# Hybrid encoder layer on one core: attention biases laid out on the host, values split before scratch, and a list scheduler that counts a shared path

## The chip, the cores and the metric

One core of a Trainium2 chip runs the whole layer. The metric is device time in microseconds (us) of one execution; lower is better. The time before is the median of three runs, 1893.22 us.

Engine names: PE multiplies matrices (PEld is its weight load), DVE is VectorE, ACT is ScalarE, POOL is GpSimd, SP is the engine whose queue issues the DMAs. SBUF is the on-chip memory, PSUM holds the results of PE in eight banks of 512 float32 columns.

## The reference, cut to what matters

Two sequences, p (512 tokens) and s (1024 tokens), pass through one encoder layer with the same weights. Tokens stand on a grid 64 columns wide, so p has 8 rows and s has 16.

```python
n = rms_norm(x, ln1_g) * (1 + sc1) + sh1
z = n @ w_in
q, k, v, xl, gl = jnp.split(z, [D_ATT, 2 * D_ATT, 3 * D_ATT, 3 * D_ATT + D_LRU], axis=-1)
...
# a query (row r, column c) sees 8 rows by 16 columns of keys
bias = rpb[:, dr[None, :, None], dc[:, None, :]]
s = einsum(q, kw) * scale + bias
p = softmax(s); att = einsum(p, vw)
...
# recurrence on xl, forward and backward, with gates; then
x = x + g1 * (concatenate([att, lru]) @ w_out)
x = x + g2 * ((gelu(ug) * uv) @ w_down)   # ug, uv: n2 @ w_up, convolved over tokens
```

There are 8 attention heads of 64, taken in 4 pairs; the feed-forward width is 2816, taken as 22 blocks of 128.

## The kernel before, in words

**Products.** Operands are float32r (a float32 of fewer mantissa bits that PE takes at full rate). Each operand is split into a high part, a copy rounded to float32r, and a low part, the operand less the high part, and a product is three matmuls (`mm3`). A split is thus two instructions per operand, a copy (ACT or DVE) and a subtraction (DVE or POOL), by `split` (line 481).

**Stages.** For each pair of heads, `qkv` (line 907) projects 128 tokens at a time to q, k and v; `lru` (958) does the recurrence; `attend` (1033) does the attention of the pair before, woven in with the projections. This fills about 95 to 851 us, together with the output projection. Then `up` (1331) makes the 22 blocks of the feed-forward inner width by a scheme of seven products for a 2x2 block product, and the down projection (from line 1417) does the same over five chunks of the inner width. In both, the sums of blocks that go into the seven products (`a_terms` 1168, `b_term` 1321) are element-wise work on DVE or POOL, and each sum is split.

**Attention before.** The bias of a pair of heads is read as one table of 16x48 per query place (`tab`, two DMAs of 384 KB for a pair). Twelve masks (0 inside the window, 1e30 outside) are read once per sequence by `masks` (1023). For each of the 8 (s) or 4 (p) query blocks and each head, a subtraction `mask - table window` makes the bias `bi` (lines 1064 to 1066), on DVE or POOL. The values v are copied from PSUM as float32, written to scratch `v_d` in HBM, read back for each column block of keys by `values(cb)` (1047), and there split into high and low part, for both heads:

```python
for hh in range(2):
    R.act(vh[:, :, hh, hh, :], v4[:, :, hh, :], AF.Copy, either=True)
    R.tt(vh[:, :, hh, 1 - hh, :], v4[:, :, hh, :], vh[:, :, hh, hh, :].bitcast(F32), ALU.subtract, pool=None)
```

**The scheduler.** The program is first recorded as a list of operations (`Recorder.op`, line 315) and then put in order by a list scheduler (`_order`, 547). Each engine has a clock; an operation takes its cost from a formula (`tt`: 2.1 ns per element and 150 on POOL, 1.045 and 67 on DVE; `mm`: columns / 2.4 and 2.5 ns). Operations with `pool=None` may go to DVE or POOL, those with `either=True` to ACT or DVE. `leave` (589) decides: an engine gives an operation up where another engine would be done before a share of its own cost is over; the shares are the table `LEAN` (line 39). The order that comes out is fixed in the program; each engine then runs its list in that order. All instructions that `_emit` makes carry line 351 in the profile, so rows are told apart by buffers: `arena_f` and `pieceNF` are float32 SBUF memory, `arena_r` and `pieceNR` float32r SBUF memory, `arena_s` small vectors, `bank` PSUM.

## Time and profile before

| what | value |
|---|---|
| median of 3 runs | 1893.22 us (1892.41 to 1893.79) |
| profiled execution, span | 1892.9 us |
| PE busy | 1721.7 us (91%), 8906 instructions |
| DVE busy | 1495.2 us (79%), 2662 |
| ACT busy | 951.8 us (50%), 1753 |
| POOL busy | 838.9 us (44%), 656 |
| DMA | 201.12 MB, mean 106 GB/s; queue 1 holds 33.2% of 16 engines |

The span is the profiled execution's own time from its first to its last instruction. Busy times of different engines overlap. An engine's busy share is an average over stages that differ, so the stages are read apart: the start (0 to 95 us), projections with attention, recurrence and output projection (95 to 851), up (851 to 1372), down with the last steps of up (1372 to 1893).

### The profile page before, as it was taken

The page shows a single profiled execution, that of the slowest core. Times are in us where ns is not written, and L with a number is a line of the kernel's source. Part 1 is how long each engine was busy: PE and PEld are TensorE (multiplying, and loading weights), DVE is VectorE, ACT ScalarE, POOL GpSimd, SP SyncE. Part 2 cuts the span into 40 slices and gives each one's busy share as a digit, 9 for nine tenths or more (in the row PEclk, how much of TensorE's full clock was granted, in tenths as well). Part 3 has the DMA queues.
Part 4 walks back from the last instruction along what each step waited for, and adds up shares of the span by engine and source line. Part 5 has one row for each costly group of instructions (what it writes and reads, how often), then busy time and mean ns, then how long its engine had stood idle before and what let it go on. Part 6 is the DMA issues. An engine that isn't in the chain of part 4 may idle for free. (4 is left out here: it accounts for less than half of the span.)

```text
span 1892.9 us, 26075 instructions
## 1 busy us (share of the span) xinstructions
PE 1721.7 (91%) x8906; PEld 1416.1 (75%) x8906; DVE 1495.2 (79%) x2662; ACT 951.8 (50%) x1753; POOL 838.9 (44%) x656
## 2 busy tenths in 40 slices
PE   6987979989898899897999999999999888888978
PEld 3665767768687578797888888888887666776756
DVE  5697797897969874868767767667698998789998
ACT  3365863857676741454444444444454554243332
POOL 0364332362616321334333333333255776467874
PEclk9998989999999899998999999999999999999989
DMA  9435314040406465462122221221232331324322
GB/s 369 162 101 150 123 45 134 17 163 13 167 12 189 99 195 173 139 206 79 56 71 64 62 68 62 62 73 56 66 97 81 115 106 55 95 71 143 118 97 97
DMA packets 144695, 201.12 MB, mean 106 GB/s; under 512 B 15793, under 2 KB 83505, under 8 KB 144561
## 3 DMA queue, kind: packets, MB, share of 16 engines
q1 hardware_dynamic: 144560, 199.44, 33.2%
q8 instruction: 70, 1.15, 0.3%
q14 instruction: 65, 0.52, 0.1%
HBM read 157.97 MB, written 41.44 MB: 105 GB/s over the span
## 5 line engine op out<-in xcount | busy, mean ns | idle before, releaser
L351 PE MATMUL bank<-arena_r 128*128 128x512 f32 (+3 forms) x3487 | 859.6, 379 | 58.0 <-ACT piece0F L351 11.0
L351 PEld LDWEIGHTS bank<-arena_r 128*128 128x128 f32 (+1 forms) x3487 | 632.2, 192 | 192.3 <-issue 22.0
L351 PE MATMUL bank<-arena_r,piece0R 128*128 128x512 f32 (+3 forms) x1323 | 325.2, 346 | 8.5 <-DVE piece4F L351 4.4
L351 PEld LDWEIGHTS bank<-arena_r,piece0R 128*128 128x128 f32 (+1 forms) x1323 | 230.6, 194 | 41.5 <-issue 6.3
L351 POOL TENSOR_TENSOR arena_r<-arena_f,arena_r 128x256 fp32r<-128x256 f32 (+4 forms) x172 | 189.8, 1113 | 159.1 <-ACT arena_r L351 74.1
L351 POOL TENSOR_TENSOR arena_f<-arena_f 128x512 f32<-128x512 f32 (+5 forms) x149 | 178.9, 1207 | 99.6 <-issue 42.9
L351 ACT ACTIVATE arena_r<-arena_f 128x256 fp32r<-128x256 f32 (+4 forms) x245 | 115.0, 495 | 130.8 <-PE bank L351 77.8
L351 PE MATMUL bank<-arena_r,piece2R 128*128 128x512 f32 (+1 forms) x735 | 179.5, 335 | 0.0
L351 DVE SCALAR_TENSOR_TENSOR arena_f<-bank,arena_s,arena_f 128x255 f32<-128x255 f32 (+2 forms) x308 | 157.5, 535 | 21.2 <-ACT arena_f L351 10.5
L351 ACT ACTIVATE arena_f<-arena_f,arena_s 128x384 f32<-128x384 f32 (+2 forms) x166 | 101.7, 619 | 84.7 <-DVE arena_s L351 54.4
L351 PEld LDWEIGHTS bank<-arena_r,piece2R 128*128 128x128 f32 x735 | 126.6, 190 | 16.4 <-POOL piece2R L351 0.2
L351 PE MATMUL bank<-arena_r,piece4R 128*128 128x256 f32 (+1 forms) x453 | 137.5, 330 | 0.4 <-DVE arena_f L351 0.4
L351 DVE TENSOR_TENSOR arena_f<-arena_f 128x512 f32<-128x512 f32 (+5 forms) x148 | 134.8, 919 | 3.7 <-ACT arena_f L351 2.5
L351 DVE TENSOR_TENSOR arena_r<-arena_f,arena_r 128x256 fp32r<-128x256 f32 (+5 forms) x143 | 123.8, 882 | 6.6 <-ACT arena_r L351 2.6
L351 ACT ACTIVATE arena_f<-bank 128x512 f32<-128x512 f32 (+3 forms) x186 | 82.3, 454 | 75.1 <-DVE bank L351 36.9
L351 PE MATMUL bank<-piece0R,arena_r 128*128 128x512 f32 (+3 forms) x316 | 104.4, 398 | 2.1 <-DVE arena_s L351 2.0
L351 ACT ACTIVATE piece0R<-arena_f 128x512 fp32r<-128x512 f32 (+2 forms) x78 | 48.9, 627 | 113.1 <-PE bank L351 92.5
L351 ACT ACTIVATE arena_f<-bank,arena_s 128x512 f32<-128x512 f32 (+1 forms) x132 | 89.6, 683 | 24.5 <-PE bank L351 15.2
L351 DVE TENSOR_TENSOR bank<-bank,arena_f 128x512 f32<-128x512 f32 (+1 forms) x89 | 52.3, 589 | 51.3 <-PE bank L351 32.8
L351 PEld LDWEIGHTS bank<-arena_r,piece4R 128*128 128x128 f32 x453 | 83.5, 190 | 9.3 <-issue 0.8
L351 ACT ACTIVATE piece2R<-arena_f 128x512 fp32r<-128x512 f32 x63 | 39.8, 631 | 89.9 <-PE bank L351 77.9
L351 DVE SCALAR_TENSOR_TENSOR arena_f<-arena_f,arena_s 128x511 f32<-128x511 f32 (+3 forms) x102 | 70.9, 696 | 17.4 <-ACT arena_f L351 15.4
(432 smaller groups left out, 3214.1 us busy)
## 6 DMA issues: line engine op xcount, KB each, us to landing
arena_f<-in_w_up_dram SPq DMA_DIRECT2D x96, 256.0 KB
gd<-arena_f SPq DMA_DIRECT2D x62, 256.0 KB
piece2F<-in_ada_dram SPq DMA_DIRECT2D x18, 512.0 KB
arena_f<-in_w_qkv_dram SPq DMA_DIRECT2D x24, 384.0 KB
arena_f<-gd SPq DMA_DIRECT2D x39, 192.0 KB
piece3F<-in_ada_dram SPq DMA_DIRECT2D x14, 512.0 KB
arena_f<-gd SPq DMA_DIRECT2D x46, 128.0 KB
arena_f<-in_ada_dram SPq DMA_DIRECT2D x8, 512.0 KB
```

Of the source, the lines that this page charges most:

```text
L351: fn(**{k: (v.real() if isinstance(v, View) else v) for k, v in kw.items()})
```

## The change

Three parts.

1. The host lays out the whole bias, -1e30 outside the window, as `bias_p` [4 pairs, 4 blocks, 128, 2 x 256] and `bias_s` [4, 8, 128, 2 x 384]. `attend` reads one tile per query block (256 KB for p, 384 KB for s, 48 DMAs in all), in place of 16 table DMAs and 12 mask DMAs with their 12 copies, and of 96 subtractions. The sign moves into the softmax (`scale=-1.0`).
2. `qkv` writes the values to scratch already split, [H | L | L | H] in 256 columns, from PSUM. `values` reads them straight into matmul operands. That takes away the 64 copies and 64 subtractions of `values` and adds 48 subtractions out of PSUM on DVE; the 48 copies out of PSUM stay, in another form. The scratch traffic doubles.
3. The scheduler has a resource `port`: an operation on POOL, and one on DVE whose operands are all in SBUF (other than tensor_reduce and reciprocal), starts there no earlier than the last such operation ended. `leave` compares ends with that in mind, and `LEAN` is gone. The cost of a float32r matmul becomes columns / 2.4 + 13.5 ns, at least 109.

```diff
-LEAN = {("DVE", "POOL"): 0.389, ("DVE", "DVE"): 0.536, ("ACT", "ACT"): 0.611, ("ACT", "DVE"): 1.869, ("DVE", "ACT"): 1.004}
+ONE_PORT = ("tensor_reduce", "reciprocal")
...
         o.all = {eng: (cost, emit), **dict(alts)}
+        o.port = {"POOL"} if eng == "POOL" or "POOL" in alts else set()
+        if port:
+            o.port.add("DVE")
...
-        self.op("DVE", per * n + base + (60 if ps else 0), self._emit(getattr(self.nc.vector, name), kw), reads, w, alts=alts)
+        self.op("DVE", per * n + base + (60 if ps else 0), self._emit(getattr(self.nc.vector, name), kw), reads, w, alts=alts, port=not ps and name not in ONE_PORT)
...
-            self.op("DVE", *b, [in0, in1], [out], alts={"POOL": a} if pool is None else {})
+            self.op("DVE", *b, [in0, in1], [out], alts={"POOL": a} if pool is None else {}, port=not self._ps(out, in0, in1))
...
-            cost = max(64.0, n) / 2.4 + 2.5 if rhs.ap.dtype == F32R else max(214.0, n / 0.6)
+            cost = max(max(64.0, n) / 2.4 + 13.5, 109.0) if rhs.ap.dtype == F32R else max(214.0, n / 0.6)
...
         def leave(o, e, s):
+            own = (max(s, port) if e in o.port else s) + o.alts[e][0]
             for f, (cost, _) in o.alts.items():
                 if f != e:
                     ahead = sum(ops[p].all[f][0] for c, p, v in ready[f] if c < o.key and not stale(c, p, v, f))
-                    if max(clock[f], s) + ahead + cost < s + LEAN[o.first, e] * o.alts[e][0]:
+                    if max(clock[f], s, port if f in o.port else s) + ahead + cost < own:
                         return True
             return False
...
             o.cost, emit = o.all[e]
+            if e in o.port:
+                s = max(s, port)
+                port = s + o.cost
...
-                vt = R.buf([P, 2, P], F32, "vt")
+                vt = R.buf([P, 2, 4, 64], F32R, "vt")
...
-                    R.copy(vt[:, u, :], pt[:, 256:384], either=True)
+                    v2 = pt[:, 256:384].rearrange("p (h d) -> p h d", h=2)
+                    R.act(vt[:, u, 0:4:3, :], v2, AF.Copy, either=True)
+                    R.tt(vt[:, u, 1:3, :], v2, vt[:, u, 0:4:3, :].bitcast(F32), ALU.subtract)
...
         def values(cb):
-            vr, vh = R.buf([P, nck, P], F32, "vr"), R.buf([P, nck, 2, 2, 64], F32R, "vh")
+            vh = R.buf([P, nck, 2 * P], F32R, "vh")
             for a in range(nck):
-                R.dma(vr[:, a, :], src[a, :, KB[cb]:KB[cb] + 32, :])
-            v4 = vr.rearrange("p a (h d) -> p a h d", h=2)
-            for hh in range(2):
-                R.act(vh[:, :, hh, hh, :], v4[:, :, hh, :], AF.Copy, either=True)
-                R.tt(vh[:, :, hh, 1 - hh, :], v4[:, :, hh, :], vh[:, :, hh, hh, :].bitcast(F32), ALU.subtract, pool=None)
+                R.dma(vh[:, a, :].bitcast(F32), src[a, :, KB[cb]:KB[cb] + 32, :])
             return vh
...
+                bi = R.buf([P, 2, nk], F32, "bi")
+                R.dma(bi, {"p": bias_p, "s": bias_s}[q][j, var])
                 for hh in range(2):
-                    bi = R.buf([P, nk], F32, "bi")
-                    R.tt(bi.rearrange("p (a b) -> p a b", b=32), msk[var].rearrange("p (a b) -> p a b", b=32), tbs[hh][:, a0:a0 + nr, b0:b0 + 32], ALU.subtract, pool=None)
...
-                    R.vec("tensor_tensor_reduce", e, [pS[hh], bis[hh]], in0=pS[hh], in1=bis[hh], scale=1.0, scalar=3e38, op0=ALU.add, op1=ALU.min, accum_out=mn)
+                    R.vec("tensor_tensor_reduce", e, [pS[hh], bi[:, hh, :]], in0=pS[hh], in1=bi[:, hh, :], scale=-1.0, scalar=3e38, op0=ALU.add, op1=ALU.min, accum_out=mn)
```

What the scheduler makes of it is seen only in the engines' lists. Counted over the whole program, POOL goes from 661 instructions to 499, DVE from 2664 to 2690, ACT from 1635 to 1588, SP's queue from 765 to 785; PE keeps 8764. By the part of the program that records an operation, the element-wise work on POOL goes from 187 operations to 60 in the projections, the recurrence and the attention of all pairs of heads but the last, from 145 to 84 in up, and from 266 to 303 in down. In down, DVE goes from 493 operations to 423 and ACT from 345 to 378.

On POOL, in the attention and recurrence of one pair of heads of s (`128x384` are the bias subtractions, `128x4x64` the value splits, `128x1024` the products and sums of the recurrence, `128x768` the splits of weights); before:

```order
L351 TENSOR_TENSOR arena_r<-arena_f,arena_r 128x768 x3
L351 TENSOR_TENSOR arena_f<-arena_f,piece3F 128x384 x6
L351 TENSOR_TENSOR piece1R<-piece3F,piece1R 128x4x64
L351 TENSOR_TENSOR arena_f<-piece2F,piece3F 128x384
L351 TENSOR_TENSOR piece2F<-piece2F,arena_s 128x512
L351 TENSOR_TENSOR arena_f<-piece2F,piece3F 128x384 x2
L351 TENSOR_TENSOR piece3F<-arena_f,piece3F 128x384
L351 TENSOR_TENSOR arena_r<-piece4F,arena_r 64x1024
L351 TENSOR_TENSOR piece2F<-piece2F,piece4F 128x1024 x2
L351 TENSOR_TENSOR piece4F<-piece4F,piece2F 128x1024
L351 TENSOR_TENSOR piece4F<-piece4F,piece3F 128x1024
L351 TENSOR_TENSOR piece1R<-piece4F,piece1R 128x4x64 x2
```

and in the changed program, between the same kinds of weight splits of a pair:

```order
L352 TENSOR_TENSOR arena_r<-arena_f,arena_r 128x768 x2
L352 TENSOR_TENSOR piece2F<-piece2F,arena_s 128x512
L352 TENSOR_TENSOR arena_r<-arena_f,arena_r 128x256 x2
L352 TENSOR_TENSOR arena_r<-piece2F,piece0R 128x512
L352 TENSOR_TENSOR arena_r<-arena_f,arena_r 128x768 x3
L352 TENSOR_TENSOR piece0R<-arena_f,arena_r 128x768
L352 TENSOR_TENSOR piece4F<-piece4F,arena_s 128x512
```

The bias and value instructions are gone from POOL, and the `128x1024` ones of the recurrence stand on DVE.

On DVE, in a step of up (`128x512` from arena and piece to arena_r or piece4R are splits of weights, those on `bank` the sums out of PSUM); before:

```order
L351 TENSOR_TENSOR arena_r<-arena_f,piece0R 128x512
L351 TENSOR_TENSOR arena_f<-arena_f 128x512
L351 TENSOR_TENSOR piece4R<-arena_f,piece2R 128x512
L351 TENSOR_TENSOR bank_70<-bank_70,arena_f 128x256
L351 TENSOR_TENSOR bank_72<-bank_72,arena_f 128x256
L351 TENSOR_TENSOR bank_69<-bank_69,arena_f 128x512
L351 TENSOR_TENSOR bank_71<-bank_71,arena_f 128x512
```

and now:

```order
L352 CAST arena_r<-arena_f 128x512
L352 TENSOR_TENSOR arena_r<-arena_f,arena_r 128x512
L352 TENSOR_TENSOR bank_71<-bank_71,arena_f 128x256
L352 TENSOR_TENSOR bank_73<-bank_73,arena_f 128x256
L352 CAST piece4R<-arena_f 128x512
L352 TENSOR_TENSOR bank_70<-bank_70,arena_f 128x512
L352 TENSOR_TENSOR arena_r<-arena_f,piece4R 128x512
L352 TENSOR_TENSOR bank_72<-bank_72,arena_f 128x512
L352 CAST piece4R<-arena_f 128x512
L352 TENSOR_TENSOR arena_r<-arena_f,piece4R 128x512
```

In up, DVE takes 62 copies of 512 columns from ACT and 61 subtractions from POOL, and they stand between its sums out of PSUM.

## Rows read from the trace of the kernel before

**Rows 1.** Windows by stage: length, busy us (instructions) of each engine, clock, DMA

```profile
core 0: us, PE busy (x) PEld busy (x) DVE busy (x) ACT busy (x) POOL busy (x), PEclk, DMA share, GB/s
0.00:95.00 95.00, 76.17 (x352) 46.52 (x353) 56.65 (x151) 35.77 (x57) 22.08 (x25) 0.93 0.72 265
95.00:851.00 756.00, 680.77 (x3695) 557.93 (x3694) 603.69 (x1293) 456.08 (x839) 293.41 (x210) 0.95 0.38 120
851.00:1372.00 521.00, 509.24 (x2948) 449.98 (x2947) 371.52 (x586) 243.94 (x426) 189.14 (x131) 0.99 0.22 65
1372.00:1893.00 521.00, 455.48 (x1917) 361.64 (x1915) 463.37 (x635) 216.01 (x433) 334.28 (x291) 0.96 0.31 98
```

**Rows 2.** Waits of PE, 95 to 851 us: us in total, times, longest

```profile
PE bank L351 <- DVE arena_r L351: 13.3, 11, 3.6
PE bank L470 <- issue: 8.5, 1, 8.5
PE bank L351 <- ACT piece2F L351: 7.2, 2, 5.2
...
PE bank L351 <- DVE piece0R L351: 0.6, 1, 0.6
```

**Rows 3.** Windows of one slice: two of attention, one of up, one of down

```profile
473.00:520.00 47.00, 39.56 (x235) 32.11 (x236) 46.28 (x115) 30.10 (x72) 30.07 (x23) 0.96 0.49 167
520.00:568.00 48.00, 47.40 (x254) 39.32 (x252) 32.81 (x57) 35.19 (x54) 9.44 (x4) 1.00 0.05 13
1041.00:1088.00 47.00, 47.00 (x270) 41.40 (x269) 33.43 (x58) 22.11 (x38) 16.12 (x11) 1.00 0.21 62
1750.00:1797.00 47.00, 42.35 (x174) 33.29 (x174) 46.23 (x54) 15.78 (x34) 37.79 (x30) 0.96 0.39 120
```

**Rows 4.** Timeline of DVE, 1000 to 1012 us: start, duration (us), instruction

```profile
1000.40 0.74 DVE L351 SCALAR_TENSOR_TENSOR arena_f<-bank,arena_s,arena_f 128x511 f32<-128x511 f32 x1
1001.08 1.33 DVE L351 TENSOR_TENSOR piece4R<-arena_f,piece0R 128x512 fp32r<-128x512 f32 x1
1002.33 1.78 DVE L351 TENSOR_TENSOR arena_f<-arena_f 128x512 f32<-128x512 f32 x1
1005.18 0.69 DVE L351 TENSOR_TENSOR arena_r<-arena_f,piece0R 128x512 fp32r<-128x512 f32 x1 [1.08 <-ACT piece0R L351]
```

**Rows 5.** Timeline of POOL, the same stretch

```profile
1000.56 3.00 POOL L351 TENSOR_TENSOR arena_f<-arena_f 128x512 f32<-128x512 f32 x2 [0.63 <-DVE arena_f L351]
1009.47 1.29 POOL L351 TENSOR_TENSOR piece4R<-arena_f,piece2R 128x512 fp32r<-128x512 f32 x1 [5.91 <-ACT piece2R L351]
```

**Rows 6.** Groups of DVE, 95 to 851 us: count, busy us, mean ns, idle before

```profile
L351 DVE TENSOR_SCALAR arena_f<-arena_f,arena_s 128x384 f32<-128x384 f32 x33 | 25.3, 775 | 0.2
...
L351 DVE TENSOR_TENSOR arena_f<-arena_f 128x384 f32<-128x384 bf16 x8 | 6.5, 820 | 0.1
...
L351 DVE COPY arena_f<-bank 128x128 f32<-128x128 f32 x22 | 6.0, 280 | 2.5 <-ACT piece2F L351 1.9 <-ACT piece4F L351 0.6
...
L351 DVE TENSOR_TENSOR piece2F<-arena_f 128x384 f32<-128x384 bf16 x1 | 0.5, 546 | 0.0
```

**Rows 7.** Groups of DVE, 710 to 757 us, where POOL has three instructions

```profile
L351 DVE TENSOR_TENSOR arena_f<-arena_f,piece4F 128x1024 f32<-128x1024 f32 x1 | 1.2, 1227 | 0.0
```

**Rows 8.** Groups of DVE, 0 to 47 us

```profile
L351 DVE CAST piece1R<-piece2F 128x512 fp32r<-128x512 f32 x2 | 0.8, 424 | 0.9 <-ACT piece2F L351 0.9
```

**Rows 9.** Waits of PE, 851 to 1372 us

```profile
PE bank L351 <- DVE piece4F L351: 8.1, 1, 8.1
```

**Rows 10.** Waits of PE, 1372 to 1893 us

```profile
PE bank L351 <- ACT arena_f L351: 18.0, 5, 8.0
PE bank L351 <- ACT piece0F L351: 11.0, 6, 3.9
PE bank L351 <- DVE bank L351: 10.5, 6, 2.2
```

**Rows 11.** Who waited for the table DMAs of the biases

```profile
  POOL arena_f L351: 5.1, 1
  POOL arena_r L351: 4.6, 1
```

More of the change, by code (lines that the diff above doesn't have):

```diff
@@ L208 @@
 class Op:
-    __slots__ = ("pos", "eng", "cost", "lat", "emit", "deps", "left", "users", "ready", "bufs", "aset", "start", "end", "vt", "done", "name", "alts", "all", "win", "ver", "key", "first", "move", "late", "strict")
+    __slots__ = ("pos", "eng", "cost", "lat", "emit", "deps", "left", "users", "ready", "bufs", "aset", "start", "end", "vt", "done", "name", "alts", "all", "win", "ver", "key", "first", "move", "late", "strict", "port")
 class Recorder:
@@ L312, in fixed_view, with op @@
         return self.dram(t, "fixed")
-    def op(self, eng, cost, emit, reads, writes, aset=None, lat=0.0, also=(), alts=(), move=0.0):
+    def op(self, eng, cost, emit, reads, writes, aset=None, lat=0.0, also=(), alts=(), move=0.0, port=False):
         o = Op()
@@ L372, in act @@
             alts["DVE"] = (1.045 * self._n(in_) + 127 if self._ps(in_) else 0.523 * self._n(in_) + 67, self._emit(self.nc.vector.tensor_copy, dict(out=out, in_=in_)))
-        self.op("ACT", cost, self._emit(self.nc.scalar.activation, kw), [in_, scale, bias], [out, accum_out], aset=SETS.get(func), alts=alts)
+        self.op("ACT", cost, self._emit(self.nc.scalar.activation, kw), [in_, scale, bias], [out, accum_out], aset=SETS.get(func), alts=alts, port=either and not self._ps(out, in_))
     def _act(self, out, in_, scale=None):
@@ L743, in encoder @@
 def encoder(ctx: ExitStack, tc: tile.TileContext, x_p, x_s, c_t, ada, bada, lng, w_qkv, w_xg,
-            qkg, tab, mask, lruv, gatew, w_out, w_up, w_down, ffv, y_p, y_s):
+            qkg, bias_p, bias_s, lruv, gatew, w_out, w_up, w_down, ffv, y_p, y_s):
     nc = tc.nc
@@ L790, in encoder @@
     g_d = scratch([NH, P, TP + TS], "gd")
-    v_d = {q: [scratch([s["T"], P], f"vd{q}{j}") for j in range(4)] for q, s in seqs.items()}
+    v_d = {q: [scratch([s["T"], 2 * P], f"vd{q}{j}") for j in range(4)] for q, s in seqs.items()}
     def rsqrt(ss, n, scale):
@@ L1021, in lru, with attend @@
         R.dma(cat_d[q][4 + c], h)
-    def masks(q):
-        nv, mcols, moff = (4, 256, 0) if q == "p" else (8, 384, 4 * 256)
-        out = []
-        for v in range(nv):
-            raw, m = R.buf([P, mcols], F32, "mkr"), R.buf([P, mcols], BF16, "msk")
-            R.dma(raw, mask[:, moff + v * mcols:moff + (v + 1) * mcols])
-            R.copy(m, raw)
-            out.append(m)
-        return out
-    def attend(q, msk, j, kqs):
+    def attend(q, j, kqs):
         kh, kl, qs = kqs
@@ L1293, in encoder @@
             pq, pj, pk = prev
-            if n in (1, 5):
-                msk = masks(pq)
-            weave(main, nmain, attend(pq, msk, pj, pk), 7 if pq == "p" else 15)
+            weave(main, nmain, attend(pq, pj, pk), 7 if pq == "p" else 15)
         prev = (q, j, out[0]) if out else None
@@ L1573, in _layout @@
     rpb = a["rpb"][0]
-    r, c = np.arange(8), np.arange(16)
-    ra = np.clip((np.arange(TAB_R) - 4)[None, :] - r[:, None] + 7, 0, 14)
-    cb = np.clip((np.arange(TAB_C) - 16)[None, :] - c[:, None] + 15, 0, 30)
-    t = rpb[:, ra[:, None, :, None], cb[None, :, None, :]]
-    f["tab"] = t.reshape(4, 2, P, TAB_R * TAB_C).transpose(0, 2, 1, 3)
-    f["mask"] = _masks()
+    table = np.concatenate([rpb.reshape(8, 15 * 31), np.full((8, 1), -BIG, np.float32)], axis=1)
+    for q, at in zip("ps", _places()):
+        t = table[:, at]
+        f["bias_" + q] = t.reshape(4, 2, *at.shape).transpose(0, 2, 3, 1, 4)
     cols = [a["lru_conv_w"][0][i] for i in range(4)] + [a[n][0] for n in ("lru_conv_b", "lam_f", "lam_b")]
@@ L1595, in _layout @@
     return f
-_ORDER = ["x_p", "x_s", "c_t", "ada", "bada", "lng", "w_qkv", "w_xg", "qkg", "tab", "mask", "lruv", "gatew",
+_ORDER = ["x_p", "x_s", "c_t", "ada", "bada", "lng", "w_qkv", "w_xg", "qkg", "bias_p", "bias_s", "lruv", "gatew",
           "w_out", "w_up", "w_down", "ffv"]
```

40 lines of the change are left out of this document (17 added, 23 removed).

## The prediction

> **What bounds the kernel now.** I read the windows by stage first, then the waits of PE in each stage, then single slices, then the timeline where DVE and POOL run together. The profiled execution spans 1892.9 us, 0.3 under the median of 1893.2, so the sum is made against the span and 0.3 is added at the end. PE is the engine with the most work, 1721.7 us busy, but it is not equally full. In up it is busy 509 of 521 us; from 95 to 851 it is idle for 756 - 681 = 75 us, and in down for 521 - 455 = 66 us [rows 1]. What the change can win lies in these two.
>
> From 95 to 851 the waits of PE itself add to 74.5 us. Ten rows name DVE, from 13.3 to 0.6 us, together 50.8; five name ACT, together 14.8, the largest 7.2; one of 8.5 names nothing [rows 2]. So two thirds of the idle time hang on DVE. Slices show how: where DVE is busy 46.3 of 47 us, PE gets 39.6; in the next slice DVE is busy 32.8 of 48 and PE 47.4. In up, DVE at 33.4 of 47 leaves PE without a gap [rows 3]. DVE near 70% is harmless, DVE near 98% costs PE about 7 us per slice.
>
> Much of DVE's busy time is no work. On the timeline an SBUF-only subtraction of 512 columns takes 1.33 and then 1.78 us while POOL works, and 0.69 when POOL is still; a DVE instruction that reads PSUM, beside the same POOL instruction, takes its 0.74 [rows 4]. POOL's two take 3.00 us, 1.5 each, where one alone takes 1.29 [rows 5]. So the two engines take turns on SBUF, while DVE's work out of PSUM goes on beside POOL. This is what the change now tells its scheduler.
>
> **The attention stretch, 95 to 851 us.** DVE has 150 SBUF-only groups there, 808 instructions, 438 us busy; the first has 33 at 775 ns, the last one at 546 ns, whose form elsewhere averages 820 [rows 6]. If each is priced at the fastest twentieth of its form in the trace, they need 293 us, which leaves 145 of waiting. With the least mean of a form's groups as price it would be 81, which is the low end, since those groups wait too; the high end is POOL's own 293 us there [rows 1]. I take 145: single instructions show the price best.
>
> POOL keeps 60 of 187 operations in this part. Waiting goes with POOL's instructions, so two thirds of it should go: -98 us of DVE's time. DVE's own work changes as follows. Gone: 38 bias subtractions, 30 of 384 columns at 0.55 [rows 6] and 8 shorter ones, 20 us; 25 copies and 24 subtractions of values and 12 mask copies at about the 0.28 of a 128-column copy [rows 6], 17. Added: 48 subtractions out of PSUM at 0.28, 13; 22 operations of 1024 columns from POOL at 1.23 [rows 7], 27; 18 of 512 at 0.69 [rows 4], 12; 5 of 768 at about 0.95, between the two, 5. The balance is +20. DVE would then be busy 604 - 98 + 20 = 526 of 756 us, 70%, which is the share that left PE full in up. Of the 50.8 us that hang on DVE I count 35 as gone: the chain of softmax and recurrence keeps some. The ends are 0 and the whole 75.
>
> The granted clock adds to this. It is 0.95 on average in this stretch and 1.00 in the slice where PE waits least [rows 1, 3]. With the two levels of 1.2 and 2.4 GHz, 0.95 means that a tenth of the 756 us ran at the lower, which costs 38 us of PE's work. I count half of that back, 19 us; ends 0 and 38. The Trainium skill, "TensorE: Matmul & The Clock Gate", section "HAM oscillation", says that PE's clock drops in its waits, so that the work behind a wait runs slower too, and that an order which keeps PE busy keeps the clock. By that rule alone the whole 38 would come back with the waits; the slices agree in direction, 0.96 beside 39.6 us busy and 1.00 beside 47.4.
>
> The transfers grow: 48 bias tiles (16.8 MB) for 8.4 MB of tables and masks, and twice the 9.4 MB of scratch traffic of the values, so about 18 MB more. Over 756 us that is 24 GB/s on top of 120, at a DMA share of 0.38 [rows 1]. I price it at nothing: the cover is the idle 0.62 of the queues, and the table DMAs made two waits of 5 us in all, on POOL [rows 11]. Without that cover each of the 48 would be waited for, at the 265 GB/s of the start [rows 1] 1.0 us for 256 KB and 1.5 for 384 KB: 16 + 48 = 64 us at most. SP's queue issues in order, so a bias tile that waits for free memory also holds the weight loads behind it; that is in this upper end. A gain here is left out, as only 10 us of waits named the tables, and on POOL.
>
> **Up, 851 to 1372 us.** PE is full but for 12 us, 8.1 of which is a single wait for DVE at the entry [rows 9]. DVE takes 62 copies at 0.42 [rows 8] and 61 subtractions at 0.69, 68 us in all, onto 372 [rows 1], and sheds part of its waits, since POOL gives up 61. That is at most 440 of 521, 84%. I put 0; the cover is DVE's remaining sixth. Ends -8 and what the slower rival gives.
>
> **Down, 1372 to 1893 us.** Here DVE is busy 463 and POOL 334 of 521 us [rows 1], in the worst slice 46.2 and 37.8 of 47 [rows 3], and PE waits for copies on ACT (18.0, 11.0) and sums on DVE's banks (10.5) that come late [rows 10]. The change gives POOL 37 operations more, DVE 70 less, ACT 33 more. The SBUF time that DVE and POOL share stays about equal: what leaves DVE for POOL costs more there, what leaves it for ACT costs it nothing. So this stage gains by order alone: PSUM work of DVE is set beside POOL's turns by a plan that knows of them. I take -12, a fifth of PE's 66 idle us; ends -45 (two thirds) and +22 (below).
>
> The matmul cost of 13.5 ns changes only when the scheduler believes PE to be free; it moves nothing that I can price, and is in the width of down.
>
> **Sum.** -35 (waits) - 19 (clock) + 0 (transfers) + 0 (up) - 12 (down) = -66: 1892.9 - 66 + 0.3 = 1827 us.
>
> **The rivals.**
>
> *Down gains as well.* If the plan sets down as I set the best end, -45 in place of -12: 1794 us. For it: the stage has the longest waits between DVE and POOL. Against: the shared time is not less. Chance 0.12; the forecast itself 0.52, with a range of its own of 1795 to 1858.
>
> *Down gives back.* POOL holds SBUF for 1.29 us per 512 columns where DVE would for 0.69 [rows 4, 5]; 37 operations more on POOL then lengthen the shared time by up to 37 x 0.6 = 22 us, in a stage where it is the limit. Attention gains 54, down loses 22: 1861 us. The Trainium skill, "SBUF — State Buffer", section "Who interferes with whom", says that the pair of ports is locked for a whole instruction and the loser blocks fully. By that rule the slower engine should never be given work where the pair is the bound, and the price is the full 22; the timeline agrees that a DVE instruction waits out POOL's. Chance 0.17.
>
> *VectorE becomes the wall in up: slower.* In the new list of DVE, copies and subtractions of weights stand in pairs between the sums out of PSUM. A sum that stands behind two of them is late by 1.1 us, and PE's banks with it. This decides once DVE's slices in up come over 46 of 47 us; then PE would get what it gets in down at that share, 42.4 of 47 [rows 3], and up loses 521 x 0.10 = 51 us. The rest would keep half of its gain with a VectorE that full, 33: 1893 + 51 - 33 = 1911 us. For it: +68 us of work there, and ACT, half idle, loses work. Against: 84% is not 98%. Chance 0.14.
>
> *The change does not do what it says.* The old shares may already have kept the two engines apart as well as a list in fixed order can; POOL's remaining instructions are the long ones, and the waits stay while DVE gets 20 us more and loses some chains. That leaves 1893 us. Chance 0.05.
>
> **How the numbers follow.** A difference under 0.2% (3.8 us) is about what a measurement of this kernel cannot tell from no change. Faster: 0.52 + 0.12 + 0.17 = 0.81; same 0.05; slower 0.14. The range of 1775 to 1900 holds the forecast, both milder and better cases and no change; it leaves out the slower rival and the far end of a good down stage.
>
> **What would show it.** POOL's instructions near 494 in the trace and its busy time in the attention stretch near 100 us; DVE's busy time there near 530, with 512-column subtractions close to 0.7 us; PE idle there near 40 us, clock 0.97; up still 509 to 521 busy; down with PE idle near 54. The forecast is wrong if DVE's slices in up are full, if PE waits for `in_bias` or scratch DMAs, or if down grows longer than 521 us.

## The result and the profile after

The changed kernel takes 1824.34 us (median of four runs, 1821.89 to 1826.37) against 1893.51 for the kernel before: ratio 0.9637, 95% interval 0.9623 to 0.965. The profiled execution spans 1822.5 us. The forecast was 1827 us, within 1775 to 1900.

The page of the changed kernel, span and busy time of each engine:

```profile
span 1822.5 us, 25666 instructions
PE 1705.3 (94%) x8906; PEld 1412.9 (78%) x8906; DVE 1421.5 (78%) x2688; ACT 927.2 (51%) x1706; POOL 619.8 (34%) x494
```

PE has the same 8906 matmuls. Its busy time fell by 16.4 us (1721.7 to 1705.3) and its idle time by 54 (1892.9 - 1721.7 = 171.2 before, 117.2 now). These two are the whole gain of 70.4.

Windows of the changed kernel at the boundaries of [rows 1] (the last is shorter), with the same columns:

```profile
0.00:95.00 95.00, 80.20 (x427) 54.73 (x428) 60.78 (x184) 46.27 (x76) 14.32 (x15) 1.00 0.73 265
95.00:851.00 756.00, 705.11 (x3881) 586.43 (x3880) 578.81 (x1287) 468.17 (x844) 155.29 (x97) 0.95 0.46 149
851.00:1372.00 521.00, 516.47 (x2927) 452.61 (x2925) 387.02 (x717) 211.28 (x366) 96.09 (x70) 1.00 0.22 66
1372.00:1823.00 451.00, 403.54 (x1674) 319.12 (x1674) 394.90 (x503) 201.49 (x422) 354.06 (x313) 0.96 0.33 104
```

These windows no longer hold the same work: 3881 matmuls fall in 95 to 851 us where 3695 did. So I set the boundaries again where the same matmul starts, counted from the end. The stages are then attention (95 us to the first matmul of the output projection of s), output projection, up, and down. Windows of the kernel before, at these boundaries:

```profile
95.00:713.00 618.00, 547.78 (x2947) 441.70 (x2946) 518.86 (x1160) 400.90 (x754) 252.32 (x186) 0.95 0.35 110
713.00:867.00 154.00, 146.56 (x864) 129.60 (x863) 100.76 (x151) 64.88 (x101) 51.14 (x31) 0.98 0.49 159
867.00:1497.00 630.00, 611.21 (x3364) 532.71 (x3363) 466.90 (x765) 298.56 (x538) 252.13 (x199) 0.98 0.23 71
1497.00:1893.00 396.00, 339.93 (x1388) 265.54 (x1386) 352.07 (x440) 151.68 (x306) 261.25 (x217) 0.96 0.31 99
```

and of the changed kernel:

```profile
95.00:673.00 578.00, 533.15 (x2873) 434.25 (x2872) 448.27 (x1097) 390.07 (x717) 97.64 (x60) 0.94 0.46 148
673.00:823.00 150.00, 145.59 (x861) 129.41 (x860) 105.82 (x160) 64.69 (x104) 40.93 (x27) 0.99 0.52 171
823.00:1440.00 617.00, 609.36 (x3364) 528.87 (x3364) 462.86 (x824) 258.00 (x455) 141.24 (x108) 1.00 0.21 66
1440.00:1823.00 383.00, 337.02 (x1389) 265.63 (x1387) 343.78 (x426) 168.18 (x358) 325.63 (x285) 0.96 0.35 109
```

- Attention is 40 us shorter. PE's idle time falls from 70.2 to 44.8 us. The rest is mostly that 75 matmuls more are done before 95 us (427 against 352), at a granted clock of 1.00 in place of 0.93.
- The output projection gains 4 us, up 13 (PE idle 18.8 to 7.6), down 13 (56.1 to 46.0).
- The clock in attention did not rise: 0.95 and 0.94.

Waits of PE, 95 to 851 us, changed kernel (us in total, times, longest), beside [rows 2]:

```profile
PE bank L352 <- ACT piece2F L352: 10.1, 2, 8.9
PE bank L352 <- ACT piece3F L352: 5.8, 2, 4.7
PE bank L471 <- ACT piece2F L352: 5.7, 2, 4.9
PE bank L352 <- DVE arena_s L352: 3.8, 5, 1.6
```

The largest row on DVE fell from 13.3 us to 3.8; the largest of all now names ACT. Over the same work, from 95 us to the first matmul of up, the rows that name DVE fall from 53.2 us in all to 16.7, and those that name ACT rise from 15.0 to 31.3. The 48 bias tiles delay nobody: the list under the last line is empty for those of s, shown here, and for those of p. All instructions on the bias of s:

```profile
L352 SPq DMA_DIRECT2D arena_f<-in_bias_s_dram x31: 327/422/1188, 264.9 to 561.7; - x31
L352 SPq DMA_DIRECT2D piece2F<-in_bias_s_dram x1: 482/482/482, 451.5 to 451.5; - x1
its engine sat idle before it (us, times) until:
who waited for it (us, times):
```

### The profile page after: what moved, and what is told of

Read it like the earlier page. It is cut to its first block, busy times and chain, and to the rows that moved or that the text cites. A ratio compares the mean times of both kernels' runs of the same rounds, so it can differ in the third digit from the quotient of the medians.

```text
span 1822.5 us, 25666 instructions
## 1 busy us (share of the span) xinstructions
PE 1705.3 (94%) x8906; PEld 1412.9 (78%) x8906; DVE 1421.5 (78%) x2688; ACT 927.2 (51%) x1706; POOL 619.8 (34%) x494
## 2 busy tenths in 40 slices
DMA packets 147571, 218.91 MB, mean 120 GB/s; under 512 B 16113, under 2 KB 82289, under 8 KB 147441
## 4 chain that ended last, share of the span: by engine, by line
PE 68%; DVE 12%; ACT 6%; DMA 5%; issue 5%; POOL 3%; SPq 2%; ACTq 0%; DVEq 0%; POOLq 0%
PE bank L352 65%; DVE arena_f L352 4%; DVE arena_r L352 3%; PE bank L471 2%; SPq L352 2%; DVE piece2F L352 2%; ACT arena_f L352 2%; POOL arena_r L352 1%; DVE arena_s L352 1%; ACT piece2F L352 1%; DVE piece3F L352 1%; ACT arena_r L352 1%; DMA arena_r<-vdp 1%; DVE piece4F L352 1%; ACT piece3F L352 1%
## 5 line engine op out<-in xcount | busy, mean ns | idle before, releaser
L352 PE MATMUL bank<-arena_r 128*128 128x512 f32 (+4 forms) x4169 | 995.5, 370 | 44.8 <-ACT piece0F L352 9.1
L352 PEld LDWEIGHTS bank<-arena_r 128*128 128x128 f32 (+1 forms) x4169 | 732.4, 192 | 188.8 <-issue 21.5
L352 POOL TENSOR_TENSOR arena_f<-arena_f 128x512 f32<-128x512 f32 (+3 forms) x144 | 170.8, 1191 | 432.8 <-DVE arena_f L352 173.6
L352 DVE SCALAR_TENSOR_TENSOR arena_f<-bank,arena_s,arena_f 128x511 f32<-128x511 f32 (+1 forms) x310 | 159.7, 538 | 28.1 <-ACT arena_f L352 20.1
L352 PE MATMUL bank<-arena_r,piece0R 128*128 128x512 f32 (+3 forms) x669 | 174.2, 366 | 1.8 <-ACT piece3F L352 1.1
L352 ACT ACTIVATE arena_f<-arena_f,arena_s 128x384 f32<-128x384 f32 (+3 forms) x190 | 115.3, 621 | 98.6 <-DVE arena_f L352 71.4
L352 PE MATMUL bank<-piece0R,arena_r 128*128 128x512 f32 (+5 forms) x479 | 140.6, 381 | 1.7 <-DMA arena_r<-vdp 0.8
L352 PEld LDWEIGHTS bank<-arena_r,piece0R 128*128 128x128 f32 (+1 forms) x669 | 121.1, 194 | 25.5 <-issue 7.2
L352 DVE TENSOR_TENSOR arena_r<-arena_f,arena_r 128x512 fp32r<-128x512 f32 (+5 forms) x147 | 125.2, 858 | 15.6 <-ACT arena_r L352 13.1
L352 DVE TENSOR_TENSOR arena_f<-arena_f 128x512 f32<-128x512 f32 (+4 forms) x120 | 94.8, 801 | 14.6 <-ACT arena_f L352 11.4
L352 DVE TENSOR_TENSOR bank<-bank,arena_f 128x512 f32<-128x512 f32 (+1 forms) x89 | 52.0, 587 | 23.2 <-PE bank L352 14.7
L352 DVE SCALAR_TENSOR_TENSOR arena_f<-arena_f,arena_s 128x511 f32<-128x511 f32 (+3 forms) x102 | 57.3, 562 | 11.5 <-ACT arena_f L352 10.0
```

What stands on the lines that cost most here:

```text
L352: fn(**{k: (v.real() if isinstance(v, View) else v) for k, v in kw.items()})
```

## The experiments

Two theories stood against each other. **Waits**, the prediction's own: PE idles because VectorE waits for the SBUF path behind GpSimd; take those waits away and PE's idle time goes. **Plan**: the waits cost little by themselves. What costs is that the order was made by a scheduler that does not know of them, so its instructions stand in a wrong order on each engine.

### The scheduler alone, the data alone

`sched_only` is the kernel before with part 3 of the change only; biases and values are as before.

```diff
-LEAN = {("DVE", "POOL"): 0.389, ("DVE", "DVE"): 0.536, ("ACT", "ACT"): 0.611, ("ACT", "DVE"): 1.869, ("DVE", "ACT"): 1.004}
+ONE_PORT = ("tensor_reduce", "reciprocal")
...
+            if e in o.port:
+                s = max(s, port)
+                port = s + o.cost
...
-            cost = max(64.0, n) / 2.4 + 2.5 if rhs.ap.dtype == F32R else max(214.0, n / 0.6)
+            cost = max(max(64.0, n) / 2.4 + 13.5, 109.0) if rhs.ap.dtype == F32R else max(214.0, n / 0.6)
```

> The kernel before with part 3 alone: the shared path in the clocks and in the choice of engine, no table of shares, the new matmul cost; biases and values as before. POOL keeps 180 of 187 operations in the attention part, 84 in up, 297 in down. Theory A (what the scheduler knows of the shared path wins the time): most of the 69 us, 1840 to 1855 us. Theory B (the work taken out of attention wins it, the scheduler does little): 1875 to 1890 us. Theory C (both needed, since with the biases and splits still there the path stays loaded in attention): 1855 to 1875, with the gain in up and down (some 25 us) there and attention as long as before.

Measured 1846.71 us, ratio 0.9755 (0.9733 to 0.9778): 47 us of the 69, as theory A had it.

`data_only` has parts 1 and 2 with the old scheduler: the changed kernel with these lines reversed.

> The changed kernel with the scheduler of before (table of shares, no shared path, matmul cost of 2.5 ns): parts 1 and 2 alone. POOL has 107 operations in the attention part, 146 in up, 274 in down. Theory A: at most 20 us of gain, 1873 to 1890 us. Theory B: 1825 to 1845 us. Theory C: 1845 to 1865 us, the gain of some 35 us in attention, with up and down as before.

Measured 1911.98 us, ratio 1.0093 (1.0077 to 1.011): slower, by 18 us, outside all three expected ranges. So with the scheduler of before, fewer instructions and less work on GpSimd (187 operations in attention before, 107 here) bring nothing in this order.

### Without the waits

`no_pool` is the changed kernel in which every operation with a choice between VectorE and GpSimd stays on VectorE.

```diff
-            self.op("DVE", *b, [in0, in1], [out], alts={"POOL": a} if pool is None else {}, port=not self._ps(out, in0, in1))
+            self.op("DVE", *b, [in0, in1], [out], alts={}, port=not self._ps(out, in0, in1))
```

> The changed kernel with every choice between DVE and POOL settled for DVE, so nothing can wait for the shared path. DVE then has 1147 operations in attention (1082 in the changed kernel), 930 in up (817), 761 in down (423). Theory: attention and up stay within 10 us, since DVE has room there, and DVE's SBUF instructions run at their own length (0.69 us for 512 columns); down becomes DVE's: 303 more operations at 0.4 to 0.7 us are some 150 us on top of about 270 of its own work, 420 us or more in place of 382, so 1850 to 1880 us in all. Rival (POOL does more harm than good everywhere): under 1815 us.

Measured 1961.7 us, ratio 1.0363 (1.0347 to 1.0378): both expectations missed. Down did not become the problem (398 us, where 420 or more was expected); attention and up, which were to stay within 10 us, grew by 37 and 89. Their windows:

```profile
95.00:710.00 615.00, 542.45 (x2900) 439.26 (x2899) 464.77 (x1171) 384.36 (x709) 0.00 (x0) 0.93 0.44 138
858.00:1564.00 706.00, 645.60 (x3362) 541.44 (x3362) 507.03 (x990) 243.08 (x423) 0.00 (x0) 0.96 0.19 58
```

GpSimd does nothing in attention, so VectorE waits for nobody on SBUF; it is busy 76% (464.77 of 615). PE is idle 72.5 us there, about as long as before the change (70.2). Up is 89 us longer than in the changed kernel though VectorE is busy only 72% there. The prediction had read from one good slice that 70% is harmless; it is not so in itself.

`no_port` is the changed kernel whose scheduler takes the two engines as independent, with the new matmul cost.

```diff
-                    if max(clock[f], s, port if f in o.port else s) + ahead + cost < own:
+                    if max(clock[f], s) + ahead + cost < s + o.alts[e][0]:
...
-            if e in o.port:
-                s = max(s, port)
-                port = s + o.cost
```

> The changed kernel, but the scheduler takes DVE and POOL as independent (no table of shares either; an operation goes where it ends first). It tells the shared path in the plan from the mere loss of the table and from the new matmul cost. Theory A: the plan's knowledge is what pays, so 1845 to 1875 us, the loss mostly in down, where both engines are loaded. Rival: the table of shares was what held the kernel back, and the path in the plan is worth nothing: 1820 to 1830 us.

Measured 1913.75 us, ratio 1.0113 (1.0098 to 1.0128): slower than theory A's 1845 to 1875, and the rival's 1820 to 1830 is refuted.

How long VectorE waits shows in what the same operation takes. Two groups of VectorE in attention (busy us, mean ns, idle before): 66 TENSOR_TENSOR operations on 16 columns, the same in every kernel, and TENSOR_SCALAR operations on 384 columns. In `before`, `sched_only`, the changed kernel, `no_port` and `no_pool`, one fence each:

```profile
L351 DVE TENSOR_SCALAR arena_f<-arena_f,arena_s 128x384 f32<-128x384 f32 x33 | 25.3, 775 | 0.2
...
L351 DVE TENSOR_TENSOR arena_s<-arena_s 128x16 f32<-128x16 f32 x66 | 21.1, 320 | 0.4
```

```profile
L354 DVE TENSOR_TENSOR arena_s<-arena_s 128x16 f32<-128x16 f32 x66 | 21.7, 329 | 0.3
...
L354 DVE TENSOR_SCALAR arena_f<-arena_f,arena_s 128x384 f32<-128x384 f32 x35 | 15.3, 441 | 0.2
```

```profile
L352 DVE TENSOR_TENSOR arena_s<-arena_s 128x16 f32<-128x16 f32 x66 | 13.9, 211 | 0.7
...
L352 DVE TENSOR_SCALAR arena_f<-arena_f,arena_s 128x384 f32<-128x384 f32 x26 | 10.7, 412 | 0.1
```

```profile
L352 DVE TENSOR_SCALAR arena_f<-arena_f,arena_s 128x384 f32<-128x384 f32 x35 | 17.5, 504 | 0.3
...
L352 DVE TENSOR_TENSOR arena_s<-arena_s 128x16 f32<-128x16 f32 x66 | 13.6, 206 | 0.7
```

```profile
L352 DVE TENSOR_SCALAR arena_f<-arena_f,arena_s 128x384 f32<-128x384 f32 x31 | 12.9, 415 | 0.4
...
L352 DVE TENSOR_TENSOR arena_s<-arena_s 128x16 f32<-128x16 f32 x66 | 11.3, 171 | 0.7
```

One group does not stand for all: `sched_only` has the 16-column operations as before (329 and 320 ns), but the 384-column ones almost as fast as `no_pool` (441 and 415, 775 before). So here is an estimate over all of VectorE's instructions in attention that touch SBUF alone: the time that each takes beyond the fastest twentieth of the same operation and shape in all fourteen kernels' traces, added up. Beside it stand the rows of PE's waits there that name DVE and ACT, each added up (all in us; `long_plan` is explained further down):

| kernel | VectorE waits (estimate) | PE waits for DVE | PE waits for ACT | attention |
|---|---|---|---|---|
| before | 109 | 46.0 | 14.7 | 618 |
| sched_only | 64 | 26.7 | 25.1 | 589 |
| changed kernel | 37 | 16.4 | 27.2 | 578 |
| no_port | 35 | 38.0 | 30.3 | 629 |
| long_plan | 33 | 53.4 | 23.3 | 630 |
| no_pool | 7 | 24.0 | 44.1 | 615 |

VectorE's waits do not set the length of attention. `no_port` and `long_plan` have those of the changed kernel (35 and 33, and 37), yet PE waits for VectorE two and three times as long and attention takes 51 and 52 us more. `no_pool` has next to none and stands at 615. **Waits** falls as the main cause. `sched_only` does not decide between the theories, since VectorE waits 45 us less in it: the scheduler that knows of the path also makes an order with fewer waits on it. Windows of attention of `sched_only`:

```profile
95.00:684.00 589.00, 536.69 (x2884) 430.07 (x2883) 465.99 (x1078) 407.95 (x775) 208.76 (x191) 0.94 0.36 114
```

and of `no_port`:

```profile
95.00:724.00 629.00, 559.77 (x2926) 444.48 (x2925) 469.92 (x1161) 388.98 (x713) 83.85 (x50) 0.93 0.43 137
```

VectorE is as busy in both (466 and 470 us), and GpSimd works 2.5 times as long in the shorter one. The largest row of PE's waits in `no_port`, 95 to 724 us, beside 3.8 us in the changed kernel:

```profile
PE bank L352 <- DVE arena_s L352: 17.3, 7, 6.7
```

### Each term of the scheduler

`port_only` is the kernel before with the shared path and without `LEAN`, matmul cost 2.5 ns as before (`sched_only` without its last two diff lines).

> The kernel before with the shared path in its scheduler and without the old shares, but with the old matmul cost of 2.5 ns. Its plan ends at 1738 us; the changed kernel with the old matmul cost ended 131 us after its plan. Theory (both terms are needed for a plan that holds): 1738 + 131 = about 1869, between 1855 and 1880, so half or less of the 46.7 us that both terms gave on the data of before. Rival A (the shared path alone is the gain): 1847. Rival B (the matmul cost alone): 1893.

Measured 1855.93 us, ratio 0.9808 (0.9792 to 0.9825): 37.7 us, four fifths of what both terms give on this data. That is just inside the expected range, but "half or less" was wrong. `LEAN` goes with the path in this run: no run on this data tells the two apart.

`old_mm_cost` is the changed kernel with the matmul cost of before.

```diff
-            cost = max(max(64.0, n) / 2.4 + 13.5, 109.0) if rhs.ap.dtype == F32R else max(214.0, n / 0.6)
+            cost = max(64.0, n) / 2.4 + 2.5 if rhs.ap.dtype == F32R else max(214.0, n / 0.6)
```

> The changed kernel with the old cost of a matmul in the scheduler (2.5 ns instead of 13.5 over the columns). After the first four runs the theory is: what pays is that the scheduler's clocks agree with the chip, be it on the shared path or on PE, since leaving out the shared path alone costs 90 us (1914) though less waits there. Theory A (the shared path is the part that matters): within 15 us of the changed kernel, 1820 to 1840. Theory A2 (PE's cost matters as much): 1850 to 1880, the loss in attention and up, where PE would be believed 5% faster than it is.

Measured 1880.71 us, ratio 0.9934 (0.9917 to 0.995): at the upper end of theory A2, 56 us slower than the changed kernel, 32 of them in attention (610 and 578) and 12 in the output projection. The timeline of PE shows which cost is right. Changed kernel, 999 to 1004 us (start, duration, instruction), where nothing is waited for:

```profile
999.68 0.62 PE L352 MATMUL bank<-piece3R,piece4R 128*128 128x512 f32 x2
1000.13 0.39 PE L352 MATMUL bank<-piece3R,arena_r 128*128 128x512 f32 x1
1000.36 0.62 PE L352 MATMUL bank<-arena_r,piece4R 128*128 128x512 f32 x2
1000.81 0.39 PE L352 MATMUL bank<-arena_r 128*128 128x512 f32 x1
1001.04 0.40 PE L352 MATMUL bank<-arena_r,piece4R 128*128 128x256 f32 x2
...
1002.11 0.40 PE L352 MATMUL bank<-arena_r,piece4R 128*128 128x256 f32 x2
...
1002.47 0.63 PE L352 MATMUL bank<-arena_r,piece4R 128*128 128x512 f32 x2
...
1003.86 0.62 PE L352 MATMUL bank<-arena_r,piece4R 128*128 128x512 f32 x2
```

Six matmuls of 512 columns start from 999.68 on, before that of 1001.04, and six from 1002.47 on, before that of 1003.86: 227 and 232 ns from start to start. Nine of 256 start from 1001.04 on, before that of 1002.11: 119 ns. Columns / 2.4 + 13.5 gives 227 and 120; with 2.5 it is 216 and 109. The plan holds 7690 such matmuls (of 256, 384 and 512 columns), so the 11 ns are 85 us by which the old plan believed PE to be early.

### Each part of the data under the new scheduler

`old_bias` has the tables, masks and subtractions of before, `old_values` the values split after scratch as before; all else is the changed kernel.

```diff
-                bi = R.buf([P, 2, nk], F32, "bi")
-                R.dma(bi, {"p": bias_p, "s": bias_s}[q][j, var])
+                    bi = R.buf([P, nk], F32, "bi")
+                    R.tt(bi.rearrange("p (a b) -> p a b", b=32), msk[var].rearrange("p (a b) -> p a b", b=32), tbs[hh][:, a0:a0 + nr, b0:b0 + 32], ALU.subtract, pool=None)
```

> The changed kernel with biases as before (tables, masks, 96 subtractions), values and scheduler as changed. sched_only is 22 us slower than the changed kernel. Theory: the 96 subtractions are the larger half of what parts 1 and 2 take away (about 24 us of DVE and 58 of POOL against about 14 and 30 for the values, by their counts and lengths): 1834 to 1846 us. Rival (it is the values): within 6 us of the changed kernel.

Measured 1888.43 us (ten runs), ratio 0.997 (0.9957 to 0.9982): missed, 42 us above the expected range.

```diff
-            vh = R.buf([P, nck, 2 * P], F32R, "vh")
+            vr, vh = R.buf([P, nck, P], F32, "vr"), R.buf([P, nck, 2, 2, 64], F32R, "vh")
...
+                R.act(vh[:, :, hh, hh, :], v4[:, :, hh, :], AF.Copy, either=True)
+                R.tt(vh[:, :, hh, 1 - hh, :], v4[:, :, hh, :], vh[:, :, hh, hh, :].bitcast(F32), ALU.subtract, pool=None)
```

> The changed kernel with values split as before at every use (float32 scratch, 64 copies and 64 subtractions), biases and scheduler as changed. Theory: the smaller half of 22 us: 1828 to 1840 us. Rival (the values' split holds the first products of each attention block, so it is the larger half): 1840 to 1850.

Measured 1834.06 us, ratio 0.9683 (0.9664 to 0.9702): as expected.

The parts don't add. Taking the bias part back costs 64 us, the values part 10, and both together, which is `sched_only`, only 22. With either part back, far more changes than the part: the scheduler makes another order of everything. So none of these numbers is the price of a part.

### Down without GpSimd

`down_no_pool` is the changed kernel in which the operations of down that have the choice stay on VectorE.

```diff
+        self.no_pool = False
...
-            self.op("DVE", *b, [in0, in1], [out], alts={"POOL": a} if pool is None else {}, port=not self._ps(out, in0, in1))
+            self.op("DVE", *b, [in0, in1], [out], alts={"POOL": a} if pool is None and not self.no_pool else {}, port=not self._ps(out, in0, in1))
...
     R.windows = None
+    R.no_pool = True
```

> The changed kernel with no work for POOL in down: its 303 operations there stand on DVE, ACT keeps about what it has. Tells whether POOL's slower hold on the shared path costs down more than its help is worth. Theory (it helps, since DVE's PSUM work runs beside it): down grows by 30 to 60 us, 1855 to 1885. Rival from the prediction (down gives back, POOL should not have the work): under 1815 us.

Measured 1819.94 us (1819.14 to 1822.44), ratio 0.9615 (0.9599 to 0.9631). Its window of down:

```profile
1438.00:1819.00 381.00, 338.82 (x1388) 262.78 (x1386) 361.84 (x727) 159.02 (x330) 0.00 (x0) 0.97 0.35 109
```

Both expectations missed: down neither grows by 30 us or more nor gives much back. GpSimd's 326 us in down were worth nothing: VectorE has 301 instructions more and is busy only 18 us more (361.8 and 343.8), and down is 2 us shorter. By the estimate used for attention, VectorE's own SBUF work in down grows from 143 to 292 us while its waits fall from 111 to 2. The median is the lowest of the study, by 4 us, but its interval overlaps that of the changed kernel.

### How far the plan tells the time

`best_plan` and `long_plan` are the changed kernel with other numbers for the scheduler. The operations are the same, but the scheduler that orders them also chooses engines: of the 2312 operations with a choice, 526 and 558 stand on another engine than in the changed kernel. VectorE has 2716 and 2744 instructions where the changed kernel has 2688, GpSimd 478 and 459 where it has 494.

```diff
-WINDOW_UP = {"PE": 44e3, "ACT": 115e3, "DVE": 115e3, "POOL": 115e3, "DMA": 82e3}
-BEST, LEAD, LAG = True, 1.275, 19e3
+WINDOW_UP = {"PE": 25.826e3, "ACT": 62.003e3, "DVE": 62.003e3, "POOL": 62.003e3, "DMA": 51.165e3}
+BEST, LEAD, LAG = True, 1.572, 14.127e3
```

> The changed kernel with four other numbers for the list scheduler (LEAD, LAG and the windows of up), so that its own plan ends at 1750 us in place of 1772; nothing else differs. Theory: with the shared path and the matmul cost in it the plan holds on the chip, and the run ends 50 to 67 us after the plan, as the four runs so far that had both did: 1800 to 1817 us. Rival (the plan's end says little; the gain was one lucky order): no link, 1815 to 1860.

Measured 1841.71 us, ratio 0.9734 (0.9705 to 0.9762): missed, 17 us slower than the changed kernel where 7 to 24 faster was expected.

```diff
-WINDOW_UP = {"PE": 44e3, "ACT": 115e3, "DVE": 115e3, "POOL": 115e3, "DMA": 82e3}
-BEST, LEAD, LAG = True, 1.275, 19e3
+WINDOW_UP = {"PE": 33.989e3, "ACT": 120.566e3, "DVE": 120.566e3, "POOL": 120.566e3, "DMA": 88.794e3}
+BEST, LEAD, LAG = True, 1.363, 21.473e3
...
-WINDOW = {"PE": 198e3, "ACT": 198e3, "DVE": 198e3, "POOL": 198e3, "DMA": 48e3}
+WINDOW = {"PE": 111.225e3, "ACT": 111.225e3, "DVE": 111.225e3, "POOL": 111.225e3, "DMA": 82.201e3}
```

> The same with numbers for which the plan ends at 1820 us, 48 later than that of the change; the instructions and their work are those of the change. Theory (time is the plan and 50 to 67 us): 1870 to 1887 us. Rival (the work on VectorE and GpSimd sets the time, the order little): near 1824, at most 1840.

Measured 1898.95 us (ten runs), ratio 1.0029 (1.0013 to 1.0045): 75 us slower than the changed kernel, by another order and choice of engines alone, and no faster than the kernel before. The rival's 1840 is refuted; the theory missed too, it had at most 1887.

`before_other` is the kernel before with LEAD 1.085 and LAG 15985.

> The kernel before with other numbers for its scheduler (LEAD 1.085, LAG 15985), its plan 7 us longer. It shows how much of a difference between two orders of the old scheduler is luck. Theory (the old plan misses by about 335 us whatever the order): 1900 us, within 15. Rival (with the old scheduler the time is a draw): off by 20 or more either way.

Measured 1892.71 us, ratio 0.9997 (0.9987 to 1.0008): no difference from before, and the rival of a draw found no support in this one order.

Part of what `best_plan` lost can be seen. PE has one wait of 21 us in it, up to 627 us, for a copy on ACT. Its timeline of PE there:

```profile
627.49 0.80 PE L352 MATMUL bank<-piece1R,arena_r 128*128 128x512 f32 x1 [21.17 <-ACT piece3F L352]
```

The timeline of ACT just before:

```profile
600.80 1.06 ACT L352 ACTIVATE arena_r<-piece3F 64x1024 fp32r<-64x1024 f32 x1
621.77 1.06 ACT L352 ACTIVATE arena_r<-piece3F 128x1024 fp32r<-128x1024 f32 x1 [19.91 <-DMA piece3F<-in_w_out_dram]
```

and of SP's queue:

```profile
597.41 11.47 SPq L352 DMA_DIRECT2D gd<-arena_s  x2
609.00 3.42 SPq L352 DMA_DIRECT2D piece3F<-in_w_out_dram  x3
```

ACT stands 19.9 us before a copy of output weights, whose loads were issued only at 609.00, behind two stores that hold SP's queue for 11.5 us. What held the stores the profile does not name. In the changed kernel, too, ACT stands before a copy of output weights, for 14.2 us, but PE's longest wait in the stretch is 8.9. What `best_plan` takes without this chain was not run.

The table sets the plan beside the chip. "Plan" is the scheduler's own clock for the order that it wrote, made of its cost formulas, no measured time. "Out" is the first matmul of the output projection of s, "end" the end of plan and the profiled span, all in us.

| kernel | path in plan | matmul + ns | out: plan | out: chip | late by | end: plan | end: chip |
|---|---|---|---|---|---|---|---|
| before | no | 2.5 | 555 | 713 | 158 | 1558 | 1892.9 |
| before_other | no | 2.5 | 562 | 705 | 143 | 1566 | 1890.9 |
| data_only | no | 2.5 | 576 | 733 | 157 | 1579 | 1912.5 |
| no_port | no | 13.5 | 602 | 724 | 122 | 1671 | 1912.4 |
| port_only | yes | 2.5 | 621 | 691 | 70 | 1738 | 1853.2 |
| old_mm_cost | yes | 2.5 | 617 | 705 | 88 | 1747 | 1877.3 |
| sched_only | yes | 13.5 | 622 | 684 | 62 | 1786 | 1839.2 |
| changed kernel | yes | 13.5 | 610 | 673 | 63 | 1772 | 1822.5 |
| down_no_pool | yes | 13.5 | 610 | 674 | 64 | 1752 | 1818.2 |
| old_values | yes | 13.5 | 610 | 686 | 76 | 1769 | 1835.2 |
| old_bias | yes | 13.5 | 653 | 726 | 73 | 1822 | 1884.9 |
| best_plan | yes | 13.5 | 614 | 705 | 91 | 1750 | 1841.4 |
| long_plan | yes | 13.5 | 649 | 725 | 76 | 1820 | 1892.1 |
| no_pool | yes | 13.5 | 618 | 710 | 92 | 1844 | 1961.4 |

Three things stand in it. Plans without the path reach the output projection 122 to 158 us late, plans with it 62 to 92. Plans with both terms end 51 to 118 us late, those with neither 325 to 335. And among plans that know both, the length of the plan itself differs by 94 us: the longest, at 1844, ran at 1961, the two planned at 1820 and 1822 ran at 1892 and 1885, the five at 1750 to 1786 between 1818 and 1841. Within those five, a plan's end says nothing about which is faster. So in these eight the plan's end tells apart differences of about 40 us, not of 20.

Three pairs differ in the path (the first two also in `LEAN`, which goes with it): before and `port_only` (-38), `data_only` and `old_mm_cost` (-31), `no_port` and the changed kernel (-89). All have one sign, but the sizes spread by 58 us, and the two other sets of numbers moved the changed kernel by 17 and 75. **What is shown**: with the same planner numbers, the scheduler's part makes most of the gain (47 us on the data of before; the data alone gains nothing), and the matmul cost gained nothing without the path in the plan. **What is not shown**: which of its two terms is larger. On the data of before the path gives 38 and the matmul cost then 9; on the changed data the path gives 31 and the matmul cost then 56, or, the cost first, nothing and then 89. **What stays open**: how much of the 69 us belongs to a plan that agrees with the chip, and how much to this one order being a good draw, since `long_plan` has the same scheduler and runs no faster than before; of the data's part, with 18 us slower under one scheduler and 22 faster under the other, not even the sign is shown.

## Why the prediction was right, and where not

The total was right to 3 us and the terms' places were not, so that closeness is in part luck: up to the start of up -54 was forecast and 44 us came (867 to 823), in up nothing was forecast and 13 came, and the two misses cancel.

- **Waits, -35 in 95 to 851.** From 95 us to the start of up, the same work but for 77 matmuls that are now done earlier, PE's idle time fell from 77.7 to 49.3, so -28. The size is near: the rows that name DVE fell by 36.5, where 35 was forecast, but those that name ACT rose by 16, which the sum had at nothing; a wait of 8.5 us that names nothing is gone too. VectorE's busy time there fell from 619.6 to 554.1 us, -65 where -78 was worked out, and GpSimd's from 303 to 139. The 145 us of VectorE's waiting in the forecast is somewhat high: priced by operation and shape at the fastest twentieth in that trace, the instructions need 316 of their 445 us, which leaves 129. The cause is what failed: "Waiting goes with POOL's instructions, so two thirds of it should go", and PE's idle time with it. `sched_only` kept GpSimd's instructions (191 in attention, 186 before), and by the estimate VectorE's waits there fell from 109 to 64 all the same; `no_port` lost both instructions and waits, and attention gained nothing. Why a better plan shortens PE's waits is only argued, not shown: in a list of fixed order, an instruction that is late for a reason unknown to the planner holds all that stands behind it.
- **Clock, -19 in the same stretch.** PE's busy time fell by 16.4 us in all, close to the term, but elsewhere. The granted clock of the start went from 0.93 to 1.00 and that of up from 0.98 to 1.00, that of attention from 0.95 to 0.94. The rule of the Trainium skill that was weighed there ("TensorE: Matmul & The Clock Gate", section "HAM oscillation"), that a PE kept busy keeps its clock, agrees in up, where idle time fell from 18.8 to 7.6 us. In attention it does not by the sum of the waits: PE's idle time fell by 25 us and the clock did not rise.
- **Transfers, 0.** Right: nobody waited for a bias tile, the values from scratch were waited for once by PE (0.8 us) and once by VectorE (0.7), and traffic rose by 17.8 MB (201.12 to 218.91).
- **Up, 0, and the rival with VectorE as the wall.** Up gained 13, beyond the -8 of the range for it. VectorE is busy 463 of 617 us there (75%, and 74% before), not 84%. By the estimate its own SBUF work grew by 44 us there, not 68, since other work left it, and its waits shrank by 45. `sched_only` has the same up of 616 us, so this too is the scheduler.
- **Down, -12.** It gained 13. The rival that down gives back had a price of 22 us for GpSimd holding the path. The Trainium skill, "SBUF — State Buffer", section "Who interferes with whom", gave the rule for it: the shared ports are an exclusive lock, and whoever does not get them blocks fully (the page says the latter of VectorE's two-port modes, and of an instruction with two SBUF inputs that it contends). The rows agree that VectorE waits: with GpSimd's 326 us in down taken away, its 301 instructions more cost it 18 us. But PE gains little by that; removing the contention is worth 2 us of down.
- **The matmul cost, "it moves nothing that I can price".** Wrong as far as the runs tell. Added to the path it is worth 9 us on the data of before (`port_only` and `sched_only`) and 56 on the changed data (`old_mm_cost`), and without the path nothing (`data_only` and `no_port`, 1911.98 and 1913.75, which differ in `LEAN` too). Both gains are no larger than what two sets of planner numbers moved the changed kernel by (17 and 75), so their size is not settled.
- **The change does not do what it says.** Refuted: the scheduler's part alone gains 47 us, and with the old scheduler the changed data ran at 1912.
- **The signs that it named.** GpSimd's 494 instructions and up's 516 busy us came as forecast. In 95 to 851 us the clock stayed at 0.95 instead of rising to 0.97, and PE's idle time came to 51 us instead of 40.

## What to carry to other kernels

Before fitting a planner's shares and windows, compare its plan with the trace stage by stage and give it what the trace shows, here a path that two engines share and 11 ns per matmul: in three pairs the kernel whose planner knew the path was 31 to 89 us faster. That is no guarantee, as `long_plan` shows. Removing the contention itself is another thing and may bring nothing. And when a change goes through a list scheduler, a part cannot be priced by taking it out once: the same operations, ordered and given to engines by other planner numbers, ran 75 us apart, so take several plans before a few per cent are given to a part. Last, judge how much an engine waits by all of its instructions: one group of 66 told the opposite of the rest.

## What the runs showed of the hardware

- VectorE with GpSimd silent (`no_pool`) does the 16-column operations in 171 ns and the TENSOR_SCALAR ones on 384 columns in 415; in the kernel before, beside GpSimd, they take 320 and 775 on average. 512-column subtractions in SBUF take 0.69 us alone [rows 4]. With all of GpSimd's work of down moved over, 301 instructions more cost VectorE 18 us of busy time.
- A float32r matmul with its own weight load follows the last after 227 to 232 ns at 512 columns and 119 at 256, 10 to 16 ns more than columns / 2.4 + 2.5.
- In `best_plan`, two stores took 11.5 us of SP's queue; the loads behind them were issued after that, ACT stood 19.9 us for them and PE 21.2 us for ACT.
